# A two-layer streaming encoder on one core: zero-padded score queries, earlier and ungrouped top-256 counting, weight remainders on GpSimd, window sums by halves

## The chip, the core and the metric

The kernel runs on one core of a Trainium2 chip. TensorE multiplies matrices, VectorE and ScalarE work on 128 rows at a time, GpSimd does the same more slowly and sees no PSUM, and SyncE issues the DMAs. The metric is the device time of one execution in microseconds, lower being better.

## The reference, cut to what matters

Two layers are computed for 1024 prompt rows and 32 sample rows (with 256 cached rows), width 1024, all in float32.

```python
# layer 0
a, glu, a_gate, q, k, v, b_gate, f = split(x @ w_in)       # 7 x 512, and 8 forget logits
a = silu(layer_norm(dwconv31(a * sigmoid(glu)))) * silu(a_gate)
s = q @ k.T / 8 + ck[q] - ck[k]                            # ck: running sum of log_sigmoid(f)
o = softmax(where(causal, s, -1e30)) @ v * silu(b_gate)    # 8 heads of 64
x = layer_norm(ALPHA * x + concat(a, o) @ w_out)
# layer 1
c, c_gate, q, k, v, d_gate, iq, ik, iw = split(x @ w_in)   # iq: 4 heads of 64, ik: 64, iw: 4
c = ((window_mean(c, 2 | 4 | 8 | 16) - c) @ pool_w) * scale * silu(c_gate)
score = sum_h iw[h] * relu(rope(iq[h]) @ rope(ik).T / 8)
top = top_k(where(chunk_causal, score, -1e30), 256)        # 72 of 288 for the sample rows
o = softmax over the chosen keys of (rope(q) @ rope(k).T / 8) @ v * silu(d_gate)
x = layer_norm(ALPHA * x + concat(c, o) @ w_out)
```

The rows returned are x of both groups and the new states (keys, values, forget values, convolution and pooling rows, indexer keys).

## The kernel before, in words

Everything float32 that goes through TensorE is split into an upper part (rounded to the matmul's format by ScalarE, `whi`, `pth`) and a remainder (a VectorE subtraction, `wlo`, `ptl`; line 107), and a product is three passes: upper x upper, remainder x upper, upper x remainder. A projection (`proj_steps`, line 192) takes 128 output columns: for each of four row groups (three of 256, one of 288) it runs 24 matmuls, eight at a time; after each eight it calls `tick`, which releases deferred work (`defer(n, ...)` runs n ticks later) and lets background generators run. A generator yields the price of what it has issued, and a part of the background with pace p gets p units per tick. Weights are fetched two projections ahead (`want`) and cut one ahead (`ready`), in the order of a plan. The instructions so traced get their final order on each engine from a planner, which simulates the engines with its own costs and may move an instruction ahead of others.

The stages are these. Layer 0: rows are loaded and transposed (line 668), then projections for the convolution branch, values, and gates, while VectorE runs the 31-tap convolution; then `attend(0, ...)`. Layer 0's output projection and layer norm follow, then layer 1: indexer keys and queries (line 1030 on), four value projections with the indexer's `scores` in the background, the pooling stage (twelve projections, `c_val`, `c_gate`, `s_gate` for four groups, line 1455) with two backgrounds, `radix_v` on VectorE and `radix_s` on ScalarE, which search the 256th largest score of every row bit by bit; the first query and key projection `qk1(0)` with `masking` in the background (line 1495); `attend(1, ...)`; and the output.

In `attend`, a unit is (i, e): 256 query rows i of one of a pair's two heads e. `first` computes scores: for every 512 keys one pair of matmuls into one PSUM bank, `qk_mm` (line 278). Its first matmul multiplies the 64 rows of the head's query upper part `q1` by the key's 64 rows, the second, over 128 rows, multiplies `qA` (or `qB`: remainder in one half, upper part in the other) by `kA` (`kB`), the key's upper part and remainder. VectorE adds a bias and takes the minimum (line 362), ScalarE exponentiates (line 365). In layer 0 the bias is made by GpSimd (lines 891 and 893) from `ckb`, a row of running sums broadcast to 128 partitions (line 887). `second` transposes the probabilities (line 411), splits them and multiplies them by the values (line 386). At the end of a pair of units, the output goes through `ot` (line 392), and for the first three pairs `spill` writes its two parts to DRAM. Steps of the next pair's query and key projections are merged in between.

The counting in `radix_v` takes four score tiles (columns `COL[:4]`: 384, 512, 640 and 288 wide) in two groups of two. Per bit it counts the scores over a candidate (`count`, line 1221) for each tile of a group and updates that group's threshold with three short instructions (lines 1167 to 1177 for the upper 16 bits, 1205 to 1211 for the lower), issued among the other group's counts. The mixing matmuls of the pooling branch (`mix`, line 1435) need window sums (line 1416) and their split from VectorE, and the gate (line 1436) after them is VectorE's too.

## Time and profile before

| quantity | value |
|---|---|
| time, median of 3 runs | 1373.24 us (1371.05 to 1373.4) |
| the profiled execution: time, span | 1373.61 us, 1371.9 us |
| TensorE: matmuls busy, weight loads busy | 94%, 86% of the span |
| VectorE, ScalarE, GpSimd busy | 73%, 51%, 18% |
| DMA queue's share of 16 engines | 33.3% |

A profile is of one execution; its span lacks what lies before the first and after the last instruction. Shares are means over stages with different limits, so a stage has to be read by itself. A matmul's record holds its passage through the array, and successive records overlap: their starts say how fast they follow one another. PE is TensorE, PEld its weight loads, DVE VectorE, ACT ScalarE, POOL GpSimd, SP SyncE.

### The profile page before, as it was taken

Reading aid. Unit: us, or ns where it says so; the run is one execution under the profiler, and the core shown is the slowest. Engines: PE = TensorE matmul, PEld = TensorE weight load, DVE = VectorE, ACT = ScalarE, POOL = GpSimd, SP = SyncE. Lnnn points to the kernel's source line nnn. Section 1 sums busy time; section 2 is a strip of 40 time slices with the busy share of each in tenths; the row PEclk is TensorE's granted clock in tenths of the full one; section 3 lists DMA queues with packets and bytes.
Section 4 is the critical chain, followed back from the end, with each engine's and each line's share of the span. In section 5 each row is a group of like instructions: output and inputs, shape, how many; then the busy total and the mean of one; then the engine's idle time right before and its main releaser. Section 6 shows DMA issues by size and latency. Waiting matters only on the chain. (4 is left out here: it accounts for less than half of the span.)

```text
span 1371.9 us, 25230 instructions
## 1 busy us (share of the span) xinstructions
PE 1290.8 (94%) x9341; PEld 1176.9 (86%) x9344; DVE 994.8 (73%) x2227; ACT 694.1 (51%) x1484; POOL 244.5 (18%) x529
## 2 busy tenths in 40 slices
PE   7999999999899998999999978699999999989997
PEld 6999999987787886899997778598988888868997
DVE  4699997374666666647846599995677878776467
ACT  4111232494766665512256676587356767675210
POOL 0000060003333332100021245365011000100000
PEclk9999999997999998999999998899999999999999
DMA  6113312333222356353242212123333223562502
GB/s 207 47 48 88 117 47 75 108 125 90 80 74 68 73 155 192 109 169 108 92 129 64 80 48 80 31 80 94 96 79 98 58 75 87 156 203 67 199 35 93
DMA packets 175063, 134.63 MB, mean 98 GB/s; under 512 B 37242, under 2 KB 163666, under 8 KB 174940
## 3 DMA queue, kind: packets, MB, share of 16 engines
q1 hardware_dynamic: 174940, 133.02, 33.3%
q8 instruction: 73, 1.20, 0.4%
q14 instruction: 50, 0.41, 0.1%
HBM read 85.09 MB, written 42.48 MB: 93 GB/s over the span
## 5 line engine op out<-in xcount | busy, mean ns | idle before, releaser
L841 DVE SCALAR_TENSOR_TENSOR acc<-apad,vT,acc 128x1086 f32<-128x1086 f32 x120 | 156.2, 1338 | 1.1
L107 DVE TENSOR_TENSOR ptl<-bank,pth 128x512 fp32r<-128x512 f32 (+1 forms) x160 | 99.5, 633 | 49.9 <-ACT pth L106 49.0
L207 PE MATMUL bank<-x1h,whi 128*128 128x256 f32 (+3 forms) x848 | 130.0, 293 | 0.1
L207 PE MATMUL bank<-x1h,wlo 128*128 128x256 f32 (+3 forms) x848 | 128.2, 291 | 0.0
L207 PE MATMUL bank<-x1l,whi 128*128 128x256 f32 (+3 forms) x848 | 126.9, 290 | 0.0
L365 ACT ACTIVATE s<-s,mn 128x896 f32<-128x896 f32 (+7 forms) x128 | 98.9, 773 | 51.6 <-DVE mn L362 50.7
L207 PE MATMUL bank<-x0h,whi 128*128 128x256 f32 (+1 forms) x768 | 118.5, 296 | 4.3 <-ACT whi L106 3.2
L106 ACT ACTIVATE pth<-bank 128x512 fp32r<-128x512 f32 (+1 forms) x160 | 86.4, 550 | 69.3 <-PE bank L411 67.6
L207 PEld LDWEIGHTS bank<-x1h,whi 128*128 128x128 f32 (+1 forms) x848 | 116.7, 193 | 2.0 <-issue 0.7
L207 PEld LDWEIGHTS bank<-x1h,wlo 128*128 128x128 f32 (+1 forms) x848 | 116.2, 193 | 1.0 <-issue 0.4
L207 PE MATMUL bank<-x0h,wlo 128*128 128x256 f32 (+1 forms) x768 | 115.6, 292 | 0.0
L207 PEld LDWEIGHTS bank<-x1l,whi 128*128 128x128 f32 (+1 forms) x848 | 113.9, 190 | 1.3 <-issue 0.8
L207 PE MATMUL bank<-x0l,whi 128*128 128x256 f32 (+1 forms) x768 | 113.0, 287 | 0.0
L207 PEld LDWEIGHTS bank<-x0h,whi 128*128 128x128 f32 x768 | 106.2, 197 | 5.9 <-ACT whi L106 3.5
L207 PEld LDWEIGHTS bank<-x0h,wlo 128*128 128x128 f32 x768 | 105.1, 195 | 0.6
L1260 ACT ACTIVATE jka<-sc,neg 128x768 bf16<-128x768 f32 (+2 forms) x96 | 99.7, 1038 | 8.7 <-POOL neg L1287 3.9
L207 PEld LDWEIGHTS bank<-x0l,whi 128*128 128x128 f32 x768 | 102.1, 190 | 0.5
L107 DVE TENSOR_TENSOR wlo<-wraw,whi 128x1024 fp32r<-128x1024 f32 (+2 forms) x55 | 66.9, 1216 | 48.5 <-ACT whi L106 47.4
L411 PE MATMUL bank<-ident,s 128*128 128x128 f32 x576 | 96.2, 283 | 5.3 <-DVE ptl L107 3.0
L106 ACT ACTIVATE whi<-wraw 128x1024 fp32r<-128x1024 f32 (+2 forms) x62 | 64.9, 1049 | 63.1 <-PE bank L207 37.7
L386 PE MATMUL bank<-pth,v 128*128 128x256 f32 x320 | 93.2, 309 | 1.4 <-ACT pth L106 1.4
L386 PE MATMUL bank<-ptl,v 128*128 128x256 f32 x320 | 85.0, 296 | 0.5 <-DVE ptl L107 0.5
(410 smaller groups left out, 2733.2 us busy)
## 6 DMA issues: line engine op xcount, KB each, us to landing
wraw<-in_o_w_in_dram SPq DMA_DIRECT2D x26, 512.0 KB, 4.0
wraw<-in_e_w_in_dram SPq DMA_DIRECT2D x24, 512.0 KB, 4.2
xrow<-in_x_prompt_dram SPq DMA_DIRECT2D x8, 512.0 KB, 4.5
sgd<-sgc SPq DMA_DIRECT2D x32, 128.0 KB, 1.9
out_dram<-ko SPq DMA_DIRECT2D x16, 256.0 KB, 2.5
vf<-vd SPq DMA_DIRECT2D x16, 256.0 KB, 3.0
ckb<-ckd SPq DMA_DIRECT2D x8, 512.0 KB, 9.9
sg<-sgd SPq DMA_DIRECT2D x32, 128.0 KB, 2.5
```

Of the source, the lines that this page charges most:

```text
L106: act.activation(hi, src, AF.Copy)
L107: eng.tensor_tensor(lo, src, hi.bitcast(FT), op=OP.subtract)
L207: pe.matmul(ps, w[:, k, :], x[g][:, k, :], start=i == 0, stop=i == 23)
L365: act.activation(s[:, :n], s[:, :n], AF.Exp, bias=mn[:, c:c + 1], scale=-1.0, accum_out=grp[p, i][0][:, j, e:e + 1])
L386: pe.matmul(po[:, j0 * 128:j0 * 128 + w], v2[e][:, k, :], src[:, b0:b0 + w], start=k == 0 and x == 0, stop=k == 2 * i + 1 and x == 1)
L411: pe.transpose(ps[:, c:c + 128], pt[j][:, k * 128:(k + 1) * 128], ident)
L841: dve.scalar_tensor_tensor(ac, apad[c][:, j:j + 1086], vT[:, c, j:j + 1], ac, op0=OP.mult, op1=OP.add)
L1260: act.activation(jka[:, :n], sct[COL[ND + j]], AF.Sign, bias=neg[:, j:j + 1].bitcast(FT), accum_out=cnta[:, j:j + 1])
```

## The change

It has these parts, as the diff shows below, cut to its core.

Queries. `q1` (128 rows, both heads) becomes `qz`, a tile with a plane for each head in which the other head's 64 rows are zero: GpSimd clears the two quarters (`blank_q`), ScalarE fills the other two with two copies instead of one. The first matmul of a pair then runs over 128 rows, in both layers' attention and in the indexer; the product is the same.

Layout and buffers. `ckd` is kept by head, so that a head's running sums are 4 KB in a row instead of eight pieces of 512 bytes. `ot` gets two buffers in layer 0, `sph` shares them, and `spl` has two; in layer 1 there is one of each, shared with `ot` and `rx`. `rstd`, `qr`, `trib`, the masks' `sg`, `eq`, `eqT` and the weight tiles are smaller, and `masks` lives in a pool that is opened after the pooling stage.

Start. Nine matmuls on a zeroed tile precede the rows; the first two row blocks are loaded in halves; the first weight is fetched after the second block and cut behind that block's transposes.

Counting. The scores are computed in the order of `COL` (0, 1, 2, the sample, 3, 4, 5) at pace 1.6 instead of 1.2, and `radix_v` starts as soon as the sample is scored, at pace 0.9, beside the value projections; it goes on in the pooling stage at 0.62 (0.5 before, with prices that were about half as large). Its four tiles form one group: four counts, then three updates. The count of tile 0 is pinned to its place in the program's order. `radix_s` has pace 0.55 instead of 0.62. Masks are made in the order of `COL`, with higher prices.

Weight remainders (`low`) are made on GpSimd from the value projections of layer 1 until `qk1(0)` ends. Window sums, their split and the tiles behind them are made for halves (512 and 544 columns) instead of four groups.

```diff
     def split(hi, lo, src, eng=dve, alone=False):
...
+            up = act.activation(hi, src, AF.Copy)
         eng.tensor_tensor(lo, src, hi.bitcast(FT), op=OP.subtract)
+        return up
...
+    def blank_q(pl, nm, n, **tag):
+        qz = pl.tile([128, 2, n], FR, name=nm, **tag)
+        pool.memset(qz[64:128, 0].bitcast(FT), 0.0)
+        pool.memset(qz[0:64, 1].bitcast(FT), 0.0)
+        return qz
+    def put_q(qz, qA, qB, r):
+        act.activation(qz[0:64, 0], r[0:64], AF.Copy)
+        act.activation(qz[64:128, 1], r[64:128], AF.Copy)
         act.activation(qA[64:128], r[0:64], AF.Copy)
         act.activation(qB[0:64], r[64:128], AF.Copy)
+        dve.tensor_tensor(qA[0:64], r[0:64], qz[0:64, 0].bitcast(FT), op=OP.subtract)
+        dve.tensor_tensor(qB[64:128], r[64:128], qz[64:128, 1].bitcast(FT), op=OP.subtract)
-        b = 64 * e
-        pe.matmul(ps, q1[b:b + 64, c0:c0 + m], k2[b:b + 64, k0:k0 + n], start=True, stop=False)
+        pe.matmul(ps, qz[:, e, c0:c0 + m], k2[:, k0:k0 + n], start=True, stop=False)
         pe.matmul(ps, q2[:, c0:c0 + m], k2[:, k0:k0 + n], start=False, stop=True)
...
+    def spill(l, pl, dst, src, n=256):
+        h = pl.tile([128, 256], FR, name="sph", tag="ot", bufs=2 - l)
+        lo = pl.tile([128, 256], FR, name="spl", tag=("spl", "rx")[l], bufs=2 - l)
...
-    PACE = (1.2, 0.5, 0.62)
+    PACE = (1.6, 0.62, 0.55, 0.9)
...
-                ot = ap.tile([128, 256], FT, name="ot", tag="ot", bufs=1)
+                ot = ap.tile([128, 256], FT, name="ot", tag="ot", bufs=2 - l)
...
+        still = wp.tile([128, 1040], FR, name="wlo", tag="wlo", bufs=3).bitcast(BF)[:, :512]
+        dve.memset(still, 0.0)
+        idle = ps_o()
+        for _ in range(9):
+            pe.matmul(idle, still[:, 0:128], still, start=True, stop=True)
+        start_plan(w0, [(c0 + c * 128, 128) for c in range(4) for c0 in (512, 0)])
         for t, (g, off, rows) in enumerate(TT):
...
+            if t == 1:
+                want(0)
+            up = to_xt(xt, rows, X0, t)
+            if t == 1:
+                with tc.issue_after(up.ins):
+                    ready(0)
...
-                         bass.AP(tensor=ckd.tensor, offset=ckd.offset + h * 128, ap=[[0, 128], [1024, 8], [1, 128]]))
+            sp.dma_start(ckb, bass.AP(tensor=ckd.tensor, offset=ckd.offset + h * 1408, ap=[[0, 128], [1, SEQ]]))
...
+        def count(c, b):
+            n = SCW[COL[c]]
+            x = sch[COL[c]]
+            ins = dve.tensor_scalar(jkd[:, :n], x if b > 15 else x.bitcast(U16),
+                                    (cand[:, c:c + 1].bitcast(FT) if b > 15 else cl[:, c:c + 1]), None, op0=OP.is_gt,
+                                    op1=OP.add, accum_out=cntd[:, c:c + 1])
+            if c == 0:
+                tc.keep_in_program_order(ins)
+            return 0.29 + n * 0.00104
...
+        for b in range(31, -1, -1):
+            for c in range(ND):
+                yield count(c, b)
+            for _ in lower(0, ND, b) if b < 16 else update(0, ND, cntd, ksd, b - 1):
+                pass
+            yield 0.5
+            if b == 16:
+                yield from halve(0, ND)
...
+    def when(flag, gen, pace):
+        while not flag:
+            yield pace
+        yield from gen
...
-        background((scores(), PACE[0]))
+        begun = []
+        rd, marks = when(begun, radix_v(), PACE[3]), scores()
+        low[0] = pool
+        background((marks, PACE[0]), (rd, PACE[3]))
...
-                yield 0.3 + SCW[i - 2] * 0.002
+                s3(COL[x - 2])
+                yield 0.3 + SCW[COL[x - 2]] * 0.004
...
-                defer(1, sums, c, g, cpad)
+                if g % 2:
+                    defer(1, sums, c, g // 2, cpad)
...
+        def sums(c, hf, cpad):
+            a, n = 512 * hf, (527, 574)[hf]
             src, w = cpad[:, a:a + n], 1
             for lv in range(c + 1):
+                dst = p4.tile([128, 574], FT, name=f"wb{lv % 2}", tag=f"wb{lv % 2}", bufs=2)
```

## Rows read from the trace of the kernel before

**Rows 1.** The page's row of TensorE's granted clock in 40 equal slices of 34.3 us, in tenths of full speed.

```profile
PEclk9999999997999998999999998899999999999999
```

**Rows 2.** Busy time by stage: the stretch in us from the span's start, its length, then busy us and (instructions) of each engine, the mean granted clock (PEclk), the DMA engines' share and GB/s.

```profile
core 0: us, PE busy (x) PEld busy (x) DVE busy (x) ACT busy (x) POOL busy (x), PEclk, DMA share, GB/s
0.00:36.00 36.00, 26.18 (x178) 23.70 (x179) 15.83 (x23) 17.14 (x32) 3.01 (x25) 0.91 0.63 197
36.00:280.00 244.00, 243.76 (x1948) 240.61 (x1948) 201.41 (x200) 68.14 (x132) 22.78 (x7) 1.00 0.27 76
280.00:345.00 65.00, 59.23 (x349) 51.08 (x348) 40.12 (x69) 43.89 (x81) 15.01 (x20) 0.84 0.42 114
345.00:515.00 170.00, 161.25 (x1052) 137.56 (x1050) 112.13 (x282) 114.52 (x263) 56.84 (x89) 0.96 0.34 89
...
700.00:797.00 97.00, 96.01 (x610) 78.99 (x609) 58.45 (x137) 64.96 (x145) 22.05 (x65) 1.00 0.29 81
797.00:989.00 192.00, 160.33 (x1217) 158.30 (x1216) 164.43 (x588) 119.24 (x243) 85.24 (x255) 0.90 0.24 69
989.00:1030.00 41.00, 39.66 (x325) 35.82 (x327) 29.99 (x72) 23.02 (x51) 5.95 (x4) 1.00 0.33 83
1030.00:1200.00 170.00, 166.68 (x1116) 141.75 (x1115) 135.70 (x327) 120.98 (x274) 14.69 (x11) 1.00 0.34 95
1200.00:1280.00 80.00, 74.75 (x489) 62.30 (x488) 56.95 (x147) 45.80 (x102) 1.36 (x1) 0.98 0.52 168
```

**Rows 3.** TensorE's matmuls in order of time in layer 1's attention loop: start, length (us), line, output<-inputs, array rows*columns in use and the moving tile.

```profile
1100.16 0.38 PE L386 MATMUL bank<-pth,v 128*128 128x256 f32 x1
1100.38 0.39 PE L281 MATMUL bank<-kB,qB 128*128 128x512 f32 x1
1100.62 0.28 PE L207 MATMUL bank<-x1h,wlo 128*128 128x256 f32 x1
...
1102.30 0.28 PE L386 MATMUL bank<-pth,v 128*128 128x256 f32 x1
1102.42 0.28 PE L386 MATMUL bank<-ptl,v 128*128 128x256 f32 x1
...
1108.58 0.28 PE L386 MATMUL bank<-ptl,v 128*128 128x256 f32 x1
1108.78 0.50 PE L280 MATMUL bank<-kB,q 64*128 64x512 f32 x1
1109.21 0.50 PE L281 MATMUL bank<-kB,qB 128*128 128x512 f32 x1
1109.55 0.22 PE L386 MATMUL bank<-pth,v 128*128 128x128 f32 x1
```

**Rows 4.** The instructions of line 280 (first matmul of a pair) over the whole span: count, duration in ns (least, median, most), first and last start, forms with their counts.

```profile
L280 PE MATMUL bank<-kA,q x96: 322/490/792, 309.1 to 1240.5; 64*128 64x512 f32 x48, 64*128 64x384 f32 x16, 64*128 64x128 f32 x16, 64*128 64x256 f32 x16
...
L280 PE MATMUL bank<-kiA,qi x20: 324/491/500, 712.4 to 773.1; 64*128 64x512 f32 x12, 64*128 64x384 f32 x4, 64*128 64x128 f32 x2, 64*128 64x256 f32 x2
```

**Rows 5.** All engines in order of time at the entry of layer 0's attention (SPq is SyncE issuing); in brackets the idle time before and what ended it.

```profile
309.78 1.60 SPq L887 DMA_DIRECT2D ckb<-ckd  x2
...
310.82 2.38 POOL L107 TENSOR_TENSOR wlo<-wraw,whi 128x1024 fp32r<-128x1024 f32 x1 [11.97 <-ACT whi L106]
...
311.08 2.40 DVE L275 TENSOR_TENSOR qA<-qr,q 64x256 fp32r<-64x256 f32 x1 [1.67 <-ACT q L272]
...
313.49 0.42 DVE L276 TENSOR_TENSOR qB<-qr,q 64x256 fp32r<-64x256 f32 x1
...
319.48 2.10 POOL L891 TENSOR_SCALAR s<-ckb,ncq 128x896 f32<-128x896 f32 x2 [6.27 <-DMA ckb<-ckd]
...
321.27 0.49 PE L280 MATMUL bank<-kA,q 64*128 64x512 f32 x1 [3.00 <-DVE mn L362]
```

**Rows 6.** The table of rows 2 for single microseconds: one in which a broadcast of running sums is the only load under way, one in which the layer-norm rows are broadcast (issued at 1286.35 and 1286.75).

```profile
446.00:447.00 1.00, 1.00 (x7) 1.00 (x6) 0.57 (x2) 0.19 (x1) 0.00 (x0) 0.50 0.77 62
1290.00:1291.00 1.00, 1.00 (x11) 0.97 (x11) 0.89 (x2) 0.83 (x3) 0.00 (x0) 1.00 1.01 349
```

**Rows 7.** Waits in 345 to 515: who waited for whom, us in total, times, longest.

```profile
DVE spl L107 <- DMA cod<-spl: 9.2, 2, 5.2
```

**Rows 8.** The start, engines in order of time.

```profile
4.57 1.94 PE L252 MATMUL bank<-ident,xrow 128*128 128x128 f32 x8 [4.57 <-DMA xrow<-in_x_prompt_dram]
...
5.73 0.40 SPq L112 DMA_DIRECT2D wraw<-in_e_w_in_dram  x1
...
14.06 2.08 PE L207 MATMUL bank<-x0h,whi 128*128 128x256 f32 x8 [3.21 <-ACT whi L106]
```

**Rows 9.** Waits in 797 to 989, as in rows 7.

```profile
PE bank L1435 <- DVE sgm L1436: 14.3, 3, 9.5
PE bank L1435 <- DVE plh L104: 14.0, 2, 8.7
```

**Rows 10.** VectorE's costliest groups in 797 to 989: form, count | busy us, mean ns of one | idle time before.

```profile
L1221 DVE TENSOR_SCALAR_CACHE_REDUCE wt<-sch,cl 128x384 bf16<-128x384 uint16 (+1 forms) x64 | 43.8, 685 | 0.4
...
L107 DVE TENSOR_TENSOR wlo<-wraw,whi 128x1024 fp32r<-128x1024 f32 x12 | 14.6, 1218 | 0.2 <-ACT whi L106 0.2
L1416 DVE TENSOR_TENSOR wb<-wb 128x268 f32<-128x268 f32 (+5 forms) x24 | 10.5, 442 | 0.2
...
L1207 DVE SCALAR_TENSOR_TENSOR tl<-cond,tl 128x2 f32<-128x2 f32 x32 | 5.0, 158 | 0.0
```

More of the change, by code (lines that the diff above doesn't have):

```diff
@@ L90, in tile_encoder @@
     vdS = [dp.tile([DS, 512], FT, name=f"vds{l}") for l in range(2)]
-    ckd = dp.tile([11, 8, 128], FT, name="ckd")
+    ckd = dp.tile([8, 11, 128], FT, name="ckd")
     x1d = [dp.tile([128, D], FT, name=f"x1d{t}") for t in range(9)]
@@ L316, in sgate_evac @@
         return f
-    def spill(pl, dst, src, n=256):
-        h = pl.tile([128, 256], FR, name="sph", tag="sph", bufs=1)
-        lo = pl.tile([128, 256], FR, name="spl", tag="spl", bufs=1)
+    def spill(l, pl, dst, src, n=256):
+        h = pl.tile([128, 256], FR, name="sph", tag="ot", bufs=2 - l)
+        lo = pl.tile([128, 256], FR, name="spl", tag=("spl", "rx")[l], bufs=2 - l)
         split(h[:, :n], lo[:, :n], src)
@@ L670, in tile_encoder @@
             src = A["x_prompt"][0, t * 128:(t + 1) * 128] if t < 8 else A["x_sample"][0]
-            sp.dma_start(xt[:rows], src)
-            to_xt(xt, rows, X0, t)
+            if t < 2:
+                for c0 in (0, 512):
+                    sp.dma_start(xt[:rows, c0:c0 + 512], src[:, c0:c0 + 512])
+            else:
+                sp.dma_start(xt[:rows], src)
+            if t == 1:
[4 more added lines that the diff above has]
+                    ready(0)
         vecs = ep.tile([35, 512], FT, name="vecs")
@@ L694, in tile_encoder @@
             apad.append(ap_)
-        start_plan(w0, [(c0 + c * 128, 128) for c in range(4) for c0 in (512, 0)])
         for c in range(4):
@@ L947, in tile_encoder @@
     MO = [sum(MW[:qi]) for qi in range(8)]
-    masks = lp.tile([128, sum(MW)], BF, name="masks")
     def rope_in(pl, hold, nm, g, ps, scale, rows=128):
@@ L1216, in lower @@
             yield
-        def count(c, b, *ups):
+        def count(c, b):
             n = SCW[COL[c]]
             x = sch[COL[c]]
-            dve.tensor_scalar(jkd[:, :n], x if b > 15 else x.bitcast(U16), (cand[:, c:c + 1].bitcast(FT) if b > 15 else
-                              cl[:, c:c + 1]), None, op0=OP.is_gt, op1=OP.add, accum_out=cntd[:, c:c + 1])
-            for u in ups:
-                next(u, None)
-            return 0.13 + n * 0.00052 + 0.08 * len(ups)
-        def counts(c0, c1, b, up):
-            n = c1 - c0
-            for c in range(n):
-                yield count(c0 + c, b, *[up] * (3 * (c + 1) // n - 3 * c // n))
@@ L1233, in updates @@
-        def updates(c0, c1, b):
-            if b < 16:
-                return lower(c0, c1, b)
-            return update(c0, c1, cntd[:, c0:c1], ksd[:, c0:c1], b - 1)
-        for _ in update(0, GA, None, None, 31):
+            ins = dve.tensor_scalar(jkd[:, :n], x if b > 15 else x.bitcast(U16),
[3 more added lines that the diff above has]
+                tc.keep_in_program_order(ins)
@@ L1238, in radix_v @@
+            return 0.29 + n * 0.00104
+        for _ in update(0, ND, None, None, 31):
             pass
-        b2 = update(GA, ND, None, None, 31)
         for b in range(31, -1, -1):
-            yield from counts(0, GA, b, b2)
-            b1 = updates(0, GA, b)
-            yield from counts(GA, ND, b, b1)
-            b2 = updates(GA, ND, b)
-            if b == 16:
-                for _ in b2:
-                    pass
-                yield from halve(0, GA)
-                yield from halve(GA, ND)
@@ L1359, in s3 @@
                     o0 = max(k * 128, c0)
[L1360 to L1361 removed]
+                    t0 = min(o0 - k * 128, 128)
+                    pe.matmul(ps[:, o0 - c0:cn], eqT[:w, k, :], trib[:w, t0:t0 + c0 + cn - o0], start=k == 0, stop=k == last)
             dve.tensor_scalar(nd[:, 3:4], ps[:, cn - 1:cn], 0.5, nd[:, 2:3], op0=OP.mult, op1=OP.add)
@@ L1458, in tile_encoder @@
     mctx.close()
+    rctx = ExitStack()
+    pr = rctx.enter_context(tc.tile_pool(name="pr", bufs=1, reuse_waits="tile", side="right"))
+    masks = pr.tile([128, sum(MW)], BF, name="masks")
     qctx = ExitStack()
```

420 lines of the change are left out of this document (208 added, 212 removed).

## The prediction

> **What bounds the kernel now.** I read the page's granted clock first, then a table of busy time by stage, then TensorE's own instructions in order of time, then the waits of the stages that are not full. The clock row shows slices below full speed in four places: the start, the two slices at about 300 to 340 us, one at about 515 to 550 us, and a long run from 790 to 960 us [rows 1]. The stage table says what these places are [rows 2]: TensorE is busy 243.76 of 244 us in the layer 0 projections (36 to 280), 161 of 170 and 167 of 170 in the two attention loops, 96.0 of 97 where the indexer is scored (700 to 797), but only 160 of 192 in the stage with pooling and top-256 counting (797 to 989), at a clock of 0.90, while VectorE is busy 164 of those 192. So TensorE sets the pace nearly everywhere, and VectorE does so from 797 to about 930.
>
> "Busy" hides a second thing. In the attention loop a 128-row matmul of 512 columns that stands between 128-row neighbours starts 0.22 us after the one before and is followed 0.24 us later (1100.16, 1100.38, 1100.62), and two 256-column ones start 0.12 us apart [rows 3]. Where the first of a score pair uses 64 rows, the starts are 1108.58, 1108.78, 1109.21, 1109.55: 0.20 to the 64-row one, 0.43 from it to its partner, 0.34 to the next, 0.97 in all [rows 3]. With the cadence of the undisturbed neighbours it would be 0.12 + 0.24 + 0.24 = 0.60. I read the 0.37 us as weight loads that are no longer hidden when the height of the array in use changes from 128 to 64 rows and back. The profile counts all of it as busy.
>
> **The parts of the change, one by one.** All sums start from the profiled execution, 1373.6 us (span 1371.9), which lies 0.4 us over the median of the three runs.
>
> Zero-padded queries. There are 192 pairs in the attention loops (96 with kA, as many with kB) and 40 in the indexer (20 each) [rows 4]. Each loses 0.37 us if the padded load hides: 192 x 0.37 = 71 us, 35.5 per layer, and 40 x 0.37 = 14.8 us, 86 in all. For narrow pairs (128 columns, 36 of the 232) it is less; I leave that in the range. It counts only while TensorE remains the bound. In layer 0 (345 to 515) VectorE is busy 112 and ScalarE 115 of 170 [rows 2], so there is room; I take 75%, 26 us. In layer 1 (1030 to 1200) VectorE is busy 136 of 170 [rows 2]; taking 68 of the 96 pairs as lying there (25 us), VectorE would have to be busy 136 of 145, 94%. I take 55%, 20 us. In the indexer stage VectorE is busy 58 of 97 [rows 2], but the change brings some 28 us of counting into it (below): 70%, 10 us. The padding adds one ScalarE copy per query tile (two of 64 rows where one of 128 stood): an estimate, from the 0.42 us that VectorE takes for a 64x256 operand [rows 5], of 16 x 0.4 = 7 us per layer, on an engine with 50 us free. It also adds two GpSimd memsets per tile, which no row prices; the hiding work is the rest of GpSimd's idle time, 113 of 170 us in layer 0 [rows 2], and what they cost without that cover is the rival on GpSimd's queue below.
>
> Forget rows in contiguous order (`ckd`), and two buffers for `ot`, `sph`, `spl`. At the entry of layer 0 attention two broadcast loads are issued at 309.78; GpSimd waits 6.27 us for them until 319.48, and TensorE waits 3.00 us for VectorE at 321.27 [rows 5]; the stage 280 to 345 runs at a clock of 0.84 [rows 2]. While such a load is alone the queues move 62 GB/s at a busy share of 0.77; the broadcast of the layer-norm rows, which are contiguous, moves 349 GB/s [rows 6]. So the new load should land in 2 to 4 us instead of 9 to 10; at least it is no slower. I take 7 us for the entry, between 0 and 12. The second buffer removes 9.2 us of VectorE waits (two, behind a spill's DMA) [rows 7]; after one of them the clock is at half (446 to 447) [rows 6], so I take 6, between 0 and 12. In layer 1 `sph` shares its one buffer with `ot`, and `spl` with `rx`: two new waits, of ScalarE and VectorE, for a 128 KB write; behind them are queued the exponentials and the differences. Units last several microseconds more than such a write, so I cost it at nothing; without that cover it is at most some 2 us on 12 spills. Layer 0 together: 26 + 7 + 6 = 39.
>
> The start. The first weight load is issued at 5.73, behind three row blocks and the small vectors, and the first projection matmul starts at 14.06, after a wait of 3.21 us for ScalarE's cut of that weight; the transposes began at 4.57 [rows 8], and the mean clock of 0 to 36 is 0.91 [rows 2]. Now nine idle bf16 matmuls run while rows arrive, the weights are asked for ahead of the third row block, and their cut is put behind the second block's transposes. The projection could start some 4 us sooner, but its later groups still wait for 4 MB of rows, which now queue behind 0.5 MB of weights. Between 0 and 8; I take 4.
>
> Pooling and counting (797 to 989). TensorE needs 1217 matmuls [rows 2] at 0.12 = 146 us; 192 pass. The difference of 46 is seen in two waits of the mixing matmuls for VectorE, 14.3 and 14.0 us, with single waits up to 9.5 [rows 9], plus the lower clock after each. VectorE's queue is what is late. Its load changes so. (a) Counting begins in the indexer stage: it is priced at 120 us in all (32 bits x 3.6, and 6 between the halves), and from its pace 31 steps x 0.9 = 28 of them go there, where 12% of the counts already ran; some 10 us leave this stage. (b) One group instead of two halves the updates: four updates per bit of 158 ns x 32 [rows 10] and their two-wide kin make about 26 us, 13 go. (c) Sums by halves: 24 operations of 442 ns [rows 10] and about as many others with the same width become half as many, longer ones; from nothing to half of 36 us, I take 6. (d) Twelve weight remainders of 1218 ns [rows 10] leave, 14.6 us. (e) But GpSimd's version takes 2.38 us, and a VectorE operation with two SBUF operands that met one ended with it: 2.40 us, where its twin after it took 0.42 [rows 5]. If each of the twelve blocks VectorE between 0 and 2.4 us, this is 0 to 29; the pooling stage is dense in such operations, so I take 20. In sum 164 - 10 - 13 - 6 - 15 + 20 = 140 us, just under TensorE's 146. The slower pace (0.62 per step of eight matmuls, in units that now equal microseconds: a 685 ns count [rows 10] is priced at about that) spreads the counts, so that a mixing matmul has less in front of it. Two engines at 95% do not interleave perfectly; I leave 14 us of excess: 46 - 14 = 32 us gained, between 5 and 44.
>
> The Trainium skill speaks against (d): its page "GPSIMD Engine Reference" (section 1, Specifications) says that GpSimd's SBUF interfaces are shared with VectorE, with contention for instructions with two SBUF inputs or in a two-port mode. The trace agrees for two inputs by the 2.40 us row; no row shows a count beside such an operation.
>
> Masks. Their order puts the widest three last, with doubled prices at a pace only a quarter higher, so more of them is left when the first layer 1 query projection ends. In 989 to 1030 TensorE is full now and VectorE busy 30 of 41 [rows 2]. Perhaps 10 us of masks come to stand before the attention loop on VectorE; the early units need only the first masks and TensorE has projections to fill with. Cost 5, between -2 and 12.
>
> Sum: 4 + 39 + 10 + 32 - 5 + 20 = 100; 1373.6 - 100 = **1273 us**.
>
> **The rivals.**
> VectorE stays the bound. Each moved remainder holds it the full 2.4 us, the same shared port, so the pooling stage gains 10 only; masks cost 8, the indexer gives 5, and layer 1 attention 8 since VectorE is already at 80%. 4 + 39 + 5 + 10 - 8 + 8 = 58: 1316. For it: [rows 5] and the 136 of 170. Against it: the counts, the bulk of the load, have a single tensor operand.
>
> Padding buys nothing: if the 0.37 us comes from something else in the pair (a change of weights between two accumulating matmuls), only 4 + 13 + 32 - 5 = 44 remain: 1330. Against it: the undisturbed 512-column row [rows 3], which is the partner of such a pair, displaced by another matmul. The Trainium skill has a rule on this side: "TensorE: Matmul & The Clock Gate" (Why this matters for your kernels) advises that matmuls with few rows be sliced into separate row groups, so that they run concurrently, which padding gives up. The starts 0.43 us apart show no concurrency here [rows 3].
>
> Everything lands: 86 for the pairs, 13 for layer 0's loads, 44 for pooling, 8 for the start, less 0 to 25 where VectorE fills up: 1373.6 - 151 + 0 to 25, about 1223 to 1248.
>
> GpSimd's queue stands (the slower one). In layer 0 GpSimd prepares every score tile's bias; now 16 pairs of memsets are in the same queue, and each must wait until TensorE has read the query tile that it overwrites. If the planner puts them early, all biases behind them wait, then VectorE, then TensorE. The price decides from 100 / 16 = 6.3 us per tile; at 9 us, about a unit's length, it is 144: 1373.6 - 100 + 144 = 1418. Against it: four query tiles are free to rotate, and GpSimd idles two thirds of the loop.
>
> **How the numbers follow.** The forecast, 1250 to 1300, has 0.55; VectorE bound (1300 to 1322) 0.20; padding useless (about 1330) 0.08; everything lands 0.12; GpSimd's queue 0.04; and 0.01 that the parts cancel to within the 0.2% that a measurement of this kernel can tell from no change. The range 1235 to 1325 leaves out the padding case, the slower case and half of the best one. Faster 0.94, same 0.02, slower 0.04.
>
> **What would show it.** Right: the 0.43 us after the first matmul of a pair becomes about 0.24; both attention loops shrink, layer 0 more than layer 1, with VectorE above 88% in the latter; the broadcast lands in under 5 us and the clock of 280 to 345 rises above 0.84; the pooling stage takes about 160 us with mixing waits of a few microseconds. Wrong: pairs that still take 0.97 us, VectorE two-input operations of 2.4 us all over the pooling stage, GpSimd memsets with long waits in layer 0, or TensorE idle for many microseconds between 1000 and 1040.

## The result and the profile after

The changed kernel takes **1320.93 us** (median of 4 runs, 1320.45 to 1330.75) against 1373.18: a ratio of 0.964 (95% interval 0.9594 to 0.9685). That is 52 us less, where 100 were forecast; the predicted time of 1273 was 48 us too low, though the range held the result. The profiled execution took 1320.87 us (span 1319.1).

To compare, I cut both traces at rows that both have: TensorE's first score pair of layer 0, its last value matmul there, the first score pair of the indexer, the last transpose of the values, the last mixing matmul, the first score pair of layer 1, its last value matmul. A stretch begins where the row starts; of a pair I take the second matmul.

| stretch | before, us | after, us | gained | predicted |
|---|---|---|---|---|
| start to layer 0's first pair | 309.5 | 302.9 | 6.6 | 4 |
| layer 0's attention loop | 265.4 | 228.3 | 37.1 | 39 |
| output, layer norm, to the indexer's first pair | 137.9 | 139.2 | -1.3 | 0 |
| indexer and values | 83.3 | 94.7 | **-11.4** | 10 |
| pooling and counting | 182.7 | 163.3 | 19.4 | 32 |
| masks (to layer 1's first pair) | 46.3 | 53.0 | -6.7 | -5 |
| layer 1's attention loop | 241.2 | 232.0 | 9.2 | 20 |
| rest | 105.7 | 105.7 | 0 | 0 |

Of the six terms of the sum three are near their size (start, layer 0, masks), three are not: indexer, pooling and layer 1 lack 21, 13 and 11 us. In the table of busy time by stage of the changed kernel (columns as in [rows 2]), layer 0's loop, indexer, pooling, masks, layer 1's loop:

```profile
303.00:531.00 228.00, 207.09 (x1539) 192.15 (x1538) 168.34 (x421) 169.53 (x385) 92.80 (x158) 0.98 0.38 113
...
670.00:765.00 95.00, 78.67 (x507) 70.85 (x507) 83.58 (x222) 59.48 (x132) 30.11 (x75) 0.91 0.25 67
765.00:928.00 163.00, 144.31 (x1140) 143.08 (x1141) 104.91 (x285) 115.20 (x234) 108.22 (x258) 0.94 0.26 72
928.00:981.00 53.00, 44.69 (x353) 41.96 (x353) 39.25 (x104) 21.62 (x49) 10.46 (x17) 0.90 0.33 87
981.00:1213.00 232.00, 212.51 (x1553) 191.32 (x1551) 189.48 (x470) 172.41 (x392) 25.67 (x37) 0.99 0.38 108
```

The indexer, where TensorE was busy 96.0 of 97 [rows 2], now has it busy 79 of 95 and VectorE 84. The page's clock row (slices of 33 us) shows where the low clock has gone: out of layer 0, and into four slices between 660 and 956. (The fifth, 1220 to 1253, lies in the rest, which takes as long as before.)

```profile
PEclk9999999999999999999989898999899999999899
```

**The pairs** do what was read from the rows before. TensorE in order of time, layer 0 after:

```profile
363.48 0.28 PE L395 MATMUL bank<-ptl,v 128*128 128x256 f32 x1
363.59 0.40 PE L289 MATMUL bank<-kA,qz 128*128 128x512 f32 x1
363.83 0.40 PE L290 MATMUL bank<-kA,qA 128*128 128x512 f32 x1
364.06 0.75 PE L208 MATMUL bank<-x0h,wlo 128*128 128x256 f32 x5
```

The starts are 0.11, 0.24 and 0.23 apart, 0.58 in all, where it was 0.97 [rows 3]. Over the pairs of 512 columns in layer 0's loop (44 and 43) the median goes from 0.98 to 0.58. The narrow pairs, of which the prediction says that they lose less, lose nearly as much (128 columns: 0.63 to 0.31).

TensorE's weight loads show where the 0.37 us went. Before, the pair of [rows 3], first and second matmul:

```profile
1108.78 0.18 PEld L280 LDWEIGHTS bank<-kB,q 64*128 64x128 f32 x1
1109.21 0.19 PEld L281 LDWEIGHTS bank<-kB,qB 128*128 128x128 f32 x1 [0.25 <-issue]
```

After, the pair above:

```profile
363.48 0.19 PEld L289 LDWEIGHTS bank<-kA,qz 128*128 128x128 f32 x1
363.59 0.19 PEld L290 LDWEIGHTS bank<-kA,qA 128*128 128x128 f32 x1
```

Before, each load starts together with its own matmul (1108.78 and 1109.21 in both lists); after, it starts together with the matmul ahead of its own (363.48 and 363.59) and is hidden behind that one. Over all 232 pairs the load leads its matmul by 2 ns (median, first and second) before, and by 110 and 177 ns after.

**The indexer.** Engines in order of time (L1085 is a count, L1208 adds a head to a score, L1204 is ScalarE's relu that empties the score bank, L1281 ScalarE's own counting):

```profile
711.91 0.75 DVE L1085 TENSOR_SCALAR_CACHE_REDUCE wt<-sch,cand 128x512 bf16<-128x512 bf16 x1
...
712.70 0.88 DVE L1085 TENSOR_SCALAR_CACHE_REDUCE wt<-sch,cand 128x640 bf16<-128x640 bf16 x1
...
713.50 0.48 DVE L1208 SCALAR_TENSOR_TENSOR sc<-rl,iwt,sc 128x256 f32<-128x256 f32 x1
713.90 0.51 DVE L1085 TENSOR_SCALAR_CACHE_REDUCE wt<-sch,cand 128x288 bf16<-128x288 bf16 x1
...
715.20 0.48 DVE L1208 SCALAR_TENSOR_TENSOR sc<-rl,iwt,sc 128x256 f32<-128x256 f32 x1
...
715.92 0.94 ACT L1281 ACTIVATE jka<-sc,neg 128x768 bf16<-128x768 f32 x1 [4.08 <-POOL sc L174]
...
716.85 1.06 ACT L1204 ACTIVATE rl<-bank 128x512 f32<-128x512 f32 x2
...
717.48 0.80 PE L289 MATMUL bank<-kiB,qiz 128*128 128x512 f32 x1 [3.77 <-ACT rl L1204]
```

Counts stand between the additions of a score's heads; the score is finished late, ScalarE waits 4.08 us for it (its last columns are GpSimd's to fill) with the next relu queued behind, and TensorE waits 3.77 us for the bank. By 765, 60 of the 128 counts have run (before: 18 by the same point).

**The first mixing matmul** (L1438 a window sum, L104 its upper part, L1458 the matmul):

```profile
781.93 0.38 PE L1424 MATMUL bank<-ident,cpad 128*15 128x128 f32 x2
...
789.58 0.51 DVE L1085 TENSOR_SCALAR_CACHE_REDUCE wt<-sch,cl 128x288 bf16<-128x288 uint16 x1
...
790.61 0.71 DVE L1438 TENSOR_TENSOR wb<-cpad 128x526 f32<-128x526 f32 x1
...
792.53 0.43 DVE L104 CAST plh<-pd 128x512 fp32r<-128x512 f32 x1
...
793.11 0.55 PE L1458 MATMUL bank<-plh,pwh 128*128 128x256 f32 x1 [10.80 <-DVE plh L104]
```

VectorE runs counts without a break until 790; the sums whose rows had been ready come after them, and TensorE stands 10.80 us. Then no count starts until 867: they are bunched, not spread.

**The masks** (L1316 and L1319 are VectorE's closing step of ScalarE's search, L1345 the masks' first):

```profile
937.41 1.00 DVE L1316 TENSOR_SCALAR_CACHE_REDUCE wt<-sc,thr 128x768 bf16<-128x768 f32 x1
...
942.09 0.28 PE L208 MATMUL bank<-x1l,whi 128*128 128x256 f32 x1
...
947.60 1.22 DVE L1319 CUSTOM_DVE_ANT_0 wt<-wt,sc 128x1024 f32<-128x1024 f32 x1
...
948.75 0.27 DVE L1345 TENSOR_SCALAR nd<-thr 128x1 f32<-128x1 f32 x3
...
949.99 0.50 PE L1362 MATMUL bank<-identb,eq 128*128 128x128 bf16 x3 [7.62 <-DVE nd L1348]
```

The last counts end at 937, the closing step follows, and mask transposes stand in TensorE's queue ahead of projection matmuls.

**A shared tile.** In layer 0, SyncE issuing and two engines:

```profile
336.34 0.57 SPq L298 DMA_DIRECT2D out_dram<-ko  x1
...
340.73 0.27 ACT L303 ACTIVATE kos<-bank 32x128 f32<-32x128 f32 x1 [3.45 <-DMA out_dram<-ko]
...
341.05 0.66 PE L420 MATMUL bank<-ident,s 128*128 128x128 f32 x4 [3.75 <-ACT kos L303]
```

This is an edit that the cut diff leaves out and the prediction passes over: the sample rows' key tile `kos` takes the tag `ko`, so ScalarE must wait until the 256 KB key tile has been written to DRAM, with the exponentials queued behind.

### The profile page after: what moved, and what is told of

Read it like the earlier page. It is cut to its first block, busy times and chain, and to the rows that moved or that the text cites. A ratio compares the mean times of both kernels' runs of the same rounds, so it can differ in the third digit from the quotient of the medians.

```text
span 1319.1 us, 25306 instructions
## 1 busy us (share of the span) xinstructions
PE 1216.4 (92%) x9353; PEld 1152.0 (87%) x9353; DVE 981.9 (74%) x2063; ACT 705.7 (53%) x1520; POOL 306.4 (23%) x615
## 4 chain that ended last, share of the span: by engine, by line
PE 59%; DVE 18%; ACT 10%; issue 5%; DMA 4%; POOL 3%; SPq 1%; DVEq 0%; POOLq 0%; ACTq 0%
PE bank L208 27%; PE bank L566 14%; DVE wt L1085 5%; PE bank L241 3%; PE bank L420 3%; PE bank L395 3%; ACT s L374 2%; PE bank L289 2%; ACT pth L106 1%; PE bank L290 1%; DVE sc L1208 1%; DMA rps<-rpx 1%; DVE s L371 1%; DVE ptl L107 1%; PE bank L224 1%
## 5 line engine op out<-in xcount | busy, mean ns | idle before, releaser
L208 PE MATMUL bank<-x0h,whi 128*128 128x256 f32 (+1 forms) x768 | 114.3, 289 | 1.8 <-ACT kr L805 1.0
L208 PE MATMUL bank<-x0h,wlo 128*128 128x256 f32 (+1 forms) x768 | 112.9, 288 | 0.0
L1281 ACT ACTIVATE jka<-sc,neg 128x768 bf16<-128x768 f32 (+2 forms) x96 | 99.7, 1038 | 19.7 <-POOL sc L174 8.7
L208 PEld LDWEIGHTS bank<-x0h,whi 128*128 128x128 f32 x768 | 102.1, 191 | 4.0 <-ACT kr L805 1.3
L208 PEld LDWEIGHTS bank<-x0h,wlo 128*128 128x128 f32 x768 | 102.2, 191 | 0.9
L420 PEld LDWEIGHTS bank<-ident,s 128*128 128x128 f32 x576 | 66.8, 142 | 34.7 <-DVE ptl L107 10.6
L107 POOL TENSOR_TENSOR wlo<-wraw,whi 128x1024 fp32r<-128x1024 f32 x25 | 60.6, 2422 | 149.1 <-ACT whi L106 149.0
```

The lines of the kernel that those rows point to most:

```text
L107: eng.tensor_tensor(lo, src, hi.bitcast(FT), op=OP.subtract)
L208: pe.matmul(ps, w[:, k, :], x[g][:, k, :], start=i == 0, stop=i == 23)
L420: pe.transpose(ps[:, c:c + 128], pt[j][:, k * 128:(k + 1) * 128], ident)
L1281: act.activation(jka[:, :n], sct[COL[ND + j]], AF.Sign, bias=neg[:, j:j + 1].bitcast(FT), accum_out=cnta[:, j:j + 1])
```

## The experiments

Every kernel computes the whole reference. Times are medians; ratios are to the kernel before on the same chip.

**1. Padding undone** (`q64`).

```diff
-        pe.matmul(ps, qz[:, e, c0:c0 + m], k2[:, k0:k0 + n], start=True, stop=False)
+        b = 64 * e
+        pe.matmul(ps, qz[b:b + 64, e, c0:c0 + m], k2[b:b + 64, k0:k0 + n], start=True, stop=False)
```

> The changed kernel, but the first matmul of every score pair uses again only the 64 rows of its head (the padded tile, its clears and its copies stay). Theory (the pairs' gain came in full, and was lost again elsewhere): 0.37 us per pair come back in both attention loops, 33 us in layer 0 and 19 in layer 1, little in the indexer, where TensorE waits anyway: 1365 to 1380 us, layer 0's attention from its first pair to its last value matmul about 262 instead of 228 us. Rival (layer 0 gained by its loads and buffers, the padding bought little): 1330 to 1345 us.

1353.8 us, 0.9869 (0.9841 to 0.9897): between the two. Layer 0's loop 244.8, layer 1's 246.3, the indexer 96.8. So the padding is worth 33 us in the changed kernel, 16.5 and 14.3 of it in the loops and 2 in the indexer.

**2. The counting of before** (`old_count`): its `radix_v` with two groups, started after the value projections.

```diff
-    PACE = (1.6, 0.62, 0.55, 0.9)
+    PACE = (1.6, 0.5, 0.62, 0.9)
...
-        background((marks, PACE[0]), (rd, PACE[3]))
+        background((marks, PACE[0]))
```

(Left out here: `radix_v` itself, as it was before, without the pin.)

> The changed kernel with the counting of before: two groups, begun after the value projections at the old pace and prices, unpinned. Theory (counts that run ahead of the scores and of the window sums cost the indexer stage its gain and make the stall of 11 us in the pooling stage): the indexer stage gets about 20 us shorter, the pooling stage some 10 us longer since VectorE is full there again: 1303 to 1318 us. Rival (the remainders on GpSimd hold VectorE and feed TensorE late, wherever the counts run): indexer not shorter by over 5 us, the pooling stage longer: 1325 to 1345 us.

1339.8 us, 0.9759 (0.9738 to 0.9779): the time and the stages are the rival's (indexer 98 us, pooling 186). But the run doesn't decide between the two, since it did not take away what the theory names: 64 of its 128 counts ran by the end of the indexer stage, although they are traced after it. The planner takes unpinned counts as soon as their scores are there; that the new order of the scores makes them ready early is my reading, and no run shows it by itself. The first mixing matmul then waited 21.1 us for its sums.

**3. Counts kept in their traced places** (`spread`).

```diff
-            ins = dve.tensor_scalar(jkd[:, :n], x if b > 15 else x.bitcast(U16),
+            seen = nc.cur_bb.bb.instructions
+            k = len(seen) - 1
+            while seen[k].engine != mine[0].engine or any(seen[k] is m for m in mine):
+                k -= 1
+            with tc.issue_after(seen[k]):
+              ins = dve.tensor_scalar(jkd[:, :n], x if b > 15 else x.bitcast(U16),
...
-            if c == 0:
-                tc.keep_in_program_order(ins)
```

(`mine` are the counting's own instructions: each count is ordered behind the last VectorE instruction of other work.)

> The changed kernel, each count ordered behind the last VectorE instruction of other work that was traced before it, so that no count runs ahead of its place. Theory (counts that run ahead): fewer counts beside the scores, no stall of 11 us before the first mixing matmul, the clock stays up there: 1290 to 1310 us. Rival (VectorE's total load is what counts, the order moves the wait only): 1316 to 1326 us. A third way: VectorE, strictly in order, waits for window sums with counts queued behind, and counting ends later still: 1330 us and more.

1303.6 us, 0.9499 (0.9478 to 0.9521): the theory holds. The table by stage, indexer and pooling:

```profile
674.00:757.00 83.00, 73.99 (x506) 67.69 (x505) 68.46 (x162) 58.72 (x131) 32.99 (x76) 0.94 0.28 77
757.00:910.00 153.00, 142.43 (x1146) 141.69 (x1145) 127.25 (x335) 114.61 (x234) 110.26 (x257) 0.97 0.27 77
```

The indexer takes 83.0 instead of 94.7 us, with 37 counts in it, and pooling 152.9 instead of 163.3; TensorE's wait of 10.80 us for the first window sums is gone. The change's own pin puts a tile 0 count behind the VectorE instruction traced just before; where that is the counting's own update, nothing else is held. The masks' wait stays.

**4. Remainders on VectorE** (`low_dve`).

```diff
-        low[0] = pool
         background((marks, PACE[0]), (rd, PACE[3]))
```

> The changed kernel with layer 1's weight remainders on VectorE as before. Theory (counts that run ahead): VectorE gets 20 us more work (17 remainders of 1.22 us), 6 of them beside the scores where it is full, and 15 in the pooling stage, where it idles 58 of 170: 1318 to 1332 us. Rival (each remainder on GpSimd holds VectorE up to 2 us and reaches TensorE 1.2 us later): 1296 to 1312 us.

1307.7 us, 0.9536 (0.9514 to 0.9557): the rival was right. Pooling takes 153.5 us. So the counts and the remainders are both causes, and not two names of one (run 5).

**5. Both** (`spread_low`: 3 and 4).

> Counts in their traced places, and layer 1's remainders on VectorE. Theory (both act on the same waits, before the first mixing matmul and beside the scores; once the counts are spread the remainders' place matters little): 1298 to 1306 us. Rival (two independent losses, 17 and 13 us): 1288 to 1294 us. Against both: VectorE, busy 170 of the 208 us from 757 to 965 of the spread run, gets 15 us more there and is late: 1306 to 1315 us.

1293.0 us, 0.9425 (0.9391 to 0.9458): two losses that nearly add, 17 and 11 us. The indexer goes to 79.8, pooling to 149.4.

**6. Padding on the kernel before** (`before_qz`), with the smaller tiles that make room for it.

```diff
+        pe.matmul(ps, qz[:, e, c0:c0 + m], k2[:, k0:k0 + n], start=True, stop=False)
...
-            kos = pl.tile([DS, 128], FT, name="kos", tag="kos", bufs=1)
+            kos = pl.tile([DS, 128], FT, name="kos", tag="ko", bufs=1)
```

> The kernel before with zero-padded queries in the two attention loops alone (not in the indexer); the tiles that must shrink for it are shrunk, layer 0's buffers and running sums stay as before, in layer 1 the spilled tiles share buffers as in the changed kernel. Theory (padding is worth 0.37 us per pair only where TensorE sets the pace, by the run with 64 rows 16.5 us in layer 0 and 14 in layer 1): 1338 to 1348 us. By the prediction's sizes (26 and 20 us): 1327 us. Rival (layer 0 can't use it without the second buffers and the faster loads): 1350 to 1360 us, with layer 0's loop at 260 or more of its 265 us.

1346.7 us, 0.9813 (0.9775 to 0.985), as the theory had it in sum, not in its parts: layer 0's loop 256.4 (9.0 less), layer 1's 227.4 (13.8 less). It shares `kos` too, as its diff shows, and TensorE waits 8.1 us for that tile, so the 9.0 are not the padding alone.

**7. The running sums by tile** (`old_ckd`) and **8. by head, on the kernel before** (`before_ckd`).

```diff
-    ckd = dp.tile([11, 8, 128], FT, name="ckd")
+    ckd = dp.tile([8, 11, 128], FT, name="ckd")
...
-                         bass.AP(tensor=ckd.tensor, offset=ckd.offset + h * 128, ap=[[0, 128], [1024, 8], [1, 128]]))
+            sp.dma_start(ckb, bass.AP(tensor=ckd.tensor, offset=ckd.offset + h * 1408, ap=[[0, 128], [1, SEQ]]))
```

(8 is this edit; 7 is its reverse on the changed kernel.)

> The changed kernel with the running sums kept by tile as before, so that each head's broadcast is again made of eight pieces of 512 bytes. Theory (of the 37 us that layer 0's loop gained, 16.5 are the padding and 20 the loads and buffers, the loads the larger part): layer 0's loop 8 to 14 us longer than 228, 1329 to 1336 us. Rival (the second buffers carry it, the loads are hidden but for the first): 1321 to 1326 us.

> The kernel before with the running sums kept by head alone (contiguous broadcasts), all else as before, single buffers included. Theory (the 9 us that VectorE waited for its spills were the slow broadcasts' doing, since with fast ones single buffers cost nothing): both go together, layer 0's loop 246 to 252 instead of 265 us, 1352 to 1359 us, and the waits for a spill's write under 2 us in all. Rival (the second buffers are needed for that part when TensorE runs at 64 rows): the loop 254 to 260, 1361 to 1367 us, the spill waits still 7 us and more.

Without it the changed kernel takes 1339.3 us, 0.9763 (0.9728 to 0.9797), somewhat above the range, layer 0's loop 242.3, 14.0 longer. With it alone the kernel before takes 1342.5 us, 0.9797 (0.9744 to 0.985), its loop **234.1 instead of 265.4**: more than either expectation, and most of what the whole change gains there. The waits for the broadcast and for a spill's write in `before_ckd`, then the clock of the stretches 280 to 345 and 345 to 515:

```profile
POOL s L890 <- DMA ckb<-ckd: 2.0, 1, 2.0
...
DVE spl L107 <- DMA cod<-spl: 1.6, 2, 0.9
```

```profile
280.00:345.00 65.00, 62.22 (x422) 54.66 (x420) 48.13 (x92) 52.81 (x103) 21.39 (x29) 0.97 0.40 116
345.00:515.00 170.00, 167.65 (x1104) 140.73 (x1104) 123.00 (x313) 123.48 (x282) 57.51 (x95) 1.00 0.41 126
```

The clock is 0.97 and 1.00, where it was 0.84 and 0.96 [rows 2], and the spill waits of 9.2 us [rows 7] are 1.6 with the same single buffer.

**9. Single buffers** (`bufs1`).

```diff
-        h = pl.tile([128, 256], FR, name="sph", tag="ot", bufs=2 - l)
+        h = pl.tile([128, 256], FR, name="sph", tag=("sph", "ot")[l], bufs=1)
```

(And `spl`, `ot` likewise.)

> The changed kernel with one buffer each for the output tile and the two spilled tiles in layer 0, as before. Theory (the prediction's term of 6 us, between 0 and 12): layer 0's loop 4 to 9 us longer than 228, 1325 to 1331 us. Rival (with the faster loads these writes are hidden): 1319 to 1323 us.

1320.6 us, 0.9625 (0.959 to 0.9659), loop 227.3: the second buffers are worth nothing once the loads are fast. What they are worth beside slow loads, no run shows.

**10. Own tile for `kos`** (`kos_own`), **11. the same with 64 rows** (`kos_q64`).

```diff
-            kos = pl.tile([DS, 128], FT, name="kos", tag="ko", bufs=1)
+            kos = pl.tile([DS, 128], FT, name="kos", tag=("kos", "ko")[l], bufs=1)
```

> The changed kernel with a buffer of its own for the sample rows' keys in layer 0, as before (the convolution's 1/std tile has one buffer instead of two to make room). Theory (ScalarE's wait for the key tile's write, 7 us of TensorE's time and half the clock after it, holds back the padding's gain): layer 0's loop 215 to 222 instead of 228 us, 1308 to 1315 us. Rival (the loop is at the limit of VectorE and ScalarE, the wait only moves): 225 to 228, 1318 to 1322 us.

> As the run with the own buffer, and the first matmul of each pair over 64 rows again. Theory (padding is worth the same 14 to 17 us in layer 0 as in layer 1, once nothing else holds the loop): layer 0's loop 232 to 237 us, 1340 to 1347 us. Rival (padding gains more where TensorE is free of waits, by up to the 33 us that its pairs lose): the loop 240 us and more, 1346 to 1354 us.

1309.9 us, 0.9553 (0.9533 to 0.9573), and 1342.5, 0.9797 (0.976 to 0.9834): layer 0's loop 217.4 and 235.0. The shared tile costs 11 us, and the padding is worth 17.6 in layer 0. The loop of `kos_own`, and what TensorE still waits for in it:

```profile
303.00:521.00 218.00, 204.48 (x1546) 190.00 (x1544) 167.12 (x420) 168.47 (x383) 93.29 (x158) 0.99 0.39 118
...
PE bank L289 <- DVE mn L371: 5.2, 8, 1.7
PE bank L420 <- DVE ptl L107: 4.4, 4, 1.4
```

**12 to 15. Where counting ends.** On `spread`, the mask transposes pinned behind TensorE's previous instruction (`spread_pin`). On `spread_low`, the same with the masks traced later (`mask_late`), a faster pace in pooling (`spread_low_end`), and a faster one beside the scores (`spread_low_beg`).

```diff
+                    tr = pe.transpose(pt[:w, (k - k0) * 128:(k - k0 + 1) * 128], eq[:, k * 128:k * 128 + w], identb)
+                    if k == 0:
+                        tc.keep_in_program_order(tr)        # spread_pin, mask_late
...
+                yield 0.3 + SCW[COL[x]] * 0.0008 + (6.0 if x == 0 else 0)    # mask_late
...
-    PACE = (1.6, 0.62, 0.55, 0.9)
+    PACE = (1.6, 0.74, 0.55, 0.9)                           # spread_low_end
+    PACE = (1.6, 0.62, 0.55, 1.3)                           # spread_low_beg
```

> Counts in their traced places, and the first of every four mask transposes ordered behind the TensorE instruction traced before it, so that it doesn't stand ahead of projection matmuls while the last counts run. Theory (TensorE's wait of 10 us and the half clock behind it come from the place in its queue): 1289 to 1297 us, the stretch from the last mixing matmul to layer 1's first pair 44 to 48 instead of 55 us. Rival (the masks are late anyway, and the wait moves to the first score pairs): 1300 to 1306 us.

> Spread counts, remainders on VectorE, the mask transposes traced about ten TensorE steps later and the first of every four ordered behind the TensorE instruction traced before it. Theory (TensorE waits only because of where the transposes stand in its queue): 1283 to 1289 us. Rival (masks are needed by the first score pairs, and the wait moves there): 1291 to 1300 us.

> Spread counts, remainders on VectorE, and the counting's pace in the pooling stage 0.74 instead of 0.62. Theory (the mask transposes wait 9 us because counting ends with the stage, and the closing step of ScalarE's search and the masks' first step stand behind it on VectorE): counting ends some 10 us earlier, that wait goes, with the half clock behind it: 1282 to 1288 us. Rival (denser counts delay window sums and gates as much): 1290 to 1297 us.

> Spread counts, remainders on VectorE, and the counting's pace beside the scores 1.3 instead of 0.9. Theory as for the faster end: about 10 us of counting move ahead, counting ends earlier, 1282 to 1289 us. Rival (VectorE is the bound beside the scores already, as in the changed kernel): that stage goes from 80 to over 86 us, 1292 to 1299 us.

1302.4 us, 0.9488 (0.9449 to 0.9527): no gain on `spread`, the wait is still there (11.0 us). 1293.4, 0.9434 (0.94 to 0.947): it moves, and layer 1's loop grows to 238.1. 1287.9, 0.9381 (0.9354 to 0.9407), and 1283.8, 0.9353 (0.9318 to 0.9388): the masks' stretch is 47.2 and 45.2 instead of 52.4 us (the interval of the first still touches that of `spread_low`). The wait is not one of place but of when counting ends.

**16. Cheaper masks** (`mask_cheap`, on `spread_low_beg`), **17. both paces** (`spread_low_both`), **18. the best with `kos_own`** (`beg_kos`).

```diff
-                yield 0.3 + SCW[COL[x]] * 0.0008
+                yield 0.3 + SCW[COL[x]] * 0.0004            # mask_cheap
...
-                yield 0.3 + SCW[COL[x - 2]] * 0.004
+                yield 0.3 + SCW[COL[x - 2]] * 0.002         # mask_cheap
...
+    PACE = (1.6, 0.72, 0.55, 1.3)                           # spread_low_both
```

> Spread counts, remainders on VectorE, counting at 1.3 beside the scores, and the masks' prices of before (half). Theory (the doubled prices leave mask work in layer 1's attention loop): that loop some 4 us shorter than 230, and the stretch ahead of it longer by 0 to 3: 1279 to 1284 us. Rival (the mask work delays the first projection wherever it stands): 1284 to 1290 us.

> Spread counts, remainders on VectorE, counting at 1.3 beside the scores and at 0.72 in the pooling stage. Theory (the mask wait is gone already with either; more speed only crowds the window sums): within 4 us of the run with 1.3 alone, 1280 to 1287 us. Rival (both gains add): 1274 to 1279 us.

> The best version so far (spread counts, remainders on VectorE, counting at 1.3 beside the scores) with that own buffer. Theory (layer 0's loss is independent of layer 1): 8 to 13 us less than that version's 1283.8, so 1271 to 1276 us. Rival: 1280 to 1286 us.

1283.8 us, 0.9362 (0.9322 to 0.9402): the prices put nothing into layer 1's loop (231.5). 1289.4, 0.9404 (0.9361 to 0.9447): not faster than with one (the intervals overlap), layer 1's loop 239.9, for a reason that I did not find. `beg_kos` takes **1272.1 us, 0.9282 (0.9263 to 0.9301)**, the best of all. Its layer 0 loop and pooling stage:

```profile
303.00:521.00 218.00, 203.33 (x1547) 188.61 (x1546) 166.60 (x423) 169.38 (x386) 93.11 (x158) 1.00 0.40 119
...
742.00:890.00 148.00, 142.84 (x1145) 142.08 (x1145) 132.27 (x368) 115.17 (x235) 89.13 (x245) 0.97 0.28 79
```

## Why the prediction was wrong

**The step that failed** is in the part on counting: "from its pace 31 steps x 0.9 = 28 of them go there", "some 10 us leave this stage", and with it the indexer's +10. The pace sets where a count is traced, not where it runs: the planner let them run as soon as they could, 60 of 128 beside the scores where 28 of 120 us of counting were to be, and `spread` shows the price, 12 us in the indexer and 10 in pooling. The sentence that the slower pace "spreads the counts, so that a mixing matmul has less in front of it" was false for the same reason, and right once the counts were held: pooling in `spread` gained 30 of the 32 forecast. The sum of VectorE's load (140) asked how much, where the order decided; VectorE was busy only 105 of 163 us in the stage that it held up.

That is about half of what the indexer lacks. With the counts held it takes 83.0 us, still only 0.3 less than before, where 10 were forecast; with the remainders back on VectorE as well 79.8. The padding does its part there: TensorE is busy 72 of 80 us (`spread_low`) instead of 83 of 83. But it now waits 5.4 us for ScalarE's copies of the values (`vr`), for which it never waited before. What delays these is not separated by any run.

**GpSimd's remainders** (d, e) were a gain of 15 against 20 us of VectorE held up in my sum. In all they cost 13 us (`low_dve`), 11 beside spread counts. Comparing each VectorE row that met one with the median of its form, 12 of 18 remainders in `spread` lengthen one, 18 us in sum, 11 of them in the pooling stage; in the changed kernel 9 us, 5 there. So the 20 were too many, and the cost is still larger than the 5 that the sum allowed. The rival "VectorE stays the bound" had a true mechanism, and its 1316 us came nearer than my 1273, though its stages came out otherwise (pooling gained 19 instead of 10, the indexer lost 11 instead of gaining 5). What share of the 13 is the holding, and what the later arrival at TensorE, no run here separates.

**Layer 0** came out at 37 of 39 by luck: every part of it was wrong. From run to run the loop takes 265.4 (before), 234.1 (`before_ckd`), 235.0 (`kos_q64`), 217.4 (`kos_own`), 228.3 (after). So the loads have 31.3 (7 were given), the buffers and the rest -0.9 (6), the padding 17.6 (26), the shared `kos` tile -10.9 (not seen), 37.1 in all. The shares hold for this order: taken out of the changed kernel, the new layout is worth 14.0 in the loop (`old_ckd`). The 9.2 us of spill waits belonged to the slow broadcasts, not to a missing buffer. And the entry's wait of 3.00 us [rows 5] was only the seen part. TensorE has four waits of 3 us and more in the loop of before, that one and these three (the first line has two):

```profile
PE bank L422 <- DVE ptl L107: 7.2, 2, 3.9
...
PE bank L557 <- DMA cat0h<-cod: 3.7, 1, 3.7
```

At or behind each lies a stretch at half clock (columns as in [rows 2]):

```profile
322.40:339.50 17.10, 17.10 (x53) 12.29 (x52) 6.76 (x18) 6.36 (x14) 3.13 (x7) 0.50 0.25 65
373.60:380.40 6.80, 5.33 (x21) 4.70 (x22) 4.74 (x12) 3.12 (x8) 1.21 (x3) 0.50 0.25 73
441.90:448.70 6.80, 6.41 (x27) 5.78 (x28) 4.16 (x11) 3.63 (x9) 0.13 (x1) 0.50 0.69 75
527.20:537.40 10.20, 7.70 (x25) 5.77 (x26) 2.03 (x5) 1.76 (x4) 1.12 (x2) 0.50 0.88 278
```

That is 13.8 us of waits and half of the 37 us of low clock outside them, 32 in sum; in `before_ckd` all four are gone, and its loop is 31 us shorter. The table by stage already priced much of the clock, 65 x 0.16 + 170 x 0.04 = 17 us [rows 2], more than the 7 + 6 that I took.

One sign of being wrong did show and cost next to nothing: in layer 0's loop GpSimd waits 48.5 us before its clears of the query tiles, up to 9.8 at a time. But VectorE waits for a bias 0.7 us in that loop, where it was 7.8 before, so GpSimd's queue had the room that the argument against that rival gave it.

**The padding** is right as a mechanism and too large in size: 33 us, not 56 (26 + 20 + 10). In layer 0 VectorE and ScalarE are busy 167 and 168 of 218 us (`kos_own`), and TensorE's waits for the bias step (5.2 us) and for `ptl` (4.4) stand where a part of the gain would be; that they are the reason is argued, not shown. The Trainium skill ("TensorE: Matmul & The Clock Gate", Why this matters for your kernels) advises that matmuls of few rows be sliced into separate row groups, which padding gives up. Here the partner of each 64-row matmul uses all 128 rows, and run 1 shows the opposite of a loss: padding gains 33 us.

**Layer 1** got 9 of 20: the padding has 14.3 there (run 1), and some 5 were lost to something else. It is not the shared buffers of layer 1, which the prediction put at nothing: `before_qz` has them, and gains 13.8. The loop also holds 20 matmuls of the masks that it did not hold before, but in `mask_cheap` none is left in it, and it takes 231.5. This stays open.

**The masks** cost 6.7 (5 forecast), but not through order and prices: with counting ended earlier (`spread_low_beg`) the same order and prices take 45.2 us, where it was 46.3 before, and halved prices gain nothing (run 16). The start gained 6.6 of at most 8.

## What to carry to other kernels

A pace or a place in the traced program is no place on the engine where a planner reorders: read the order on the engine's own rows, and if background work must not run ahead, order every piece behind the foreground's last instruction. Price a stall together with the low clock behind it (lost clock times length, by stage), and look for what a slow transfer makes wait elsewhere before adding buffers. And go through the tile tags of a diff one by one: here a tile of 16 KB that came to share a buffer cost 11 us.

## What was not expected of the hardware

A broadcast of 512 KB in eight pieces of 512 bytes per partition landed in 9.9 us (median), in one piece of 4 KB in 4.7 (`before_ckd`), and the slow ones also held up 128 KB writes elsewhere: 9.2 us of waits against 1.6.

A GpSimd operation can hold VectorE operations with one tensor operand, too. GpSimd and VectorE in `spread`:

```profile
723.87 2.39 POOL L107 TENSOR_TENSOR wlo<-wraw,whi 128x1024 fp32r<-128x1024 f32 x1
...
724.14 2.41 DVE L1221 TENSOR_SCALAR sc<-rl,iwt 128x512 f32<-128x512 f32 x1
```

The multiplication takes 0.48 us where nothing holds it (`old_count`). Of the counts that met a remainder in these runs none was longer. The Trainium skill ("GPSIMD Engine Reference", section 1, Specifications) names two SBUF inputs or a two-port mode; the first agrees with [rows 5], and the second would fit this row.
